# Summing the squares of the queries from 32 rows a head instead of 64

## The chip, the core and the metric

One core of a Trainium2 chip runs the whole program. The metric is the device time of one execution in microseconds. TensorE (PE) multiplies matrices, VectorE (DVE), ScalarE (ACT) and GpSimd (POOL) work element by element, and SyncE (SP) issues most of the DMA transfers. Each engine works through its own queue in order.

## The reference

One layer of an encoder over 1024 tokens of width 1024, in float32. What matters here is the start of its mixer:

```python
h = rmsnorm(x, ln1_g[l]) * (1.0 + sc1) + sh1
p = h @ w_in[l]
q, k, v, cb, cc, cx, ga, gb = jnp.split(p, split_at, axis=-1)
q = rmsnorm(q.reshape(b, s_len, SB_HEADS, SB_HEAD_DIM), q_norm_g[l])   # 16 heads of 64
...
y_a = stick_breaking_attention(q, k, v)
```

`rmsnorm` divides each head's 64 numbers by the root of the mean of their squares. Behind it come the attention, a short gated convolution, a merge by gates, an output projection and a gated feed-forward layer.

## The kernel before

A float32 product is made of three matmuls of 128 rows by 512 columns in the type `float32r`: a matrix is split into a high part (`hi`, a rounding copy by ScalarE) and the rest (`lo`, a subtraction by VectorE), and hi·hi, hi·lo and lo·hi are added up in PSUM (`half_prod`, lines 127 to 129).

The stages follow one another: the values `v` and keys `k` by tokens; then 20 "gates", each of which makes a 2x2 block of a projection by Strassen's scheme with seven products of 12 matmuls (the loop over `gates`); then the attention, with the convolution's projections as filling; the merge, the output projection and the feed-forward layer.

Gates 0 to 3 (`sec == 5`) make the queries, transposed: channels on the partitions, tokens along the columns. Gate j gives four chunks of 128 channels (two heads) by 512 tokens: `c11` is (m = j, n = 0), `c12` is (j, 1), `c21` is (j + 4, 0), `c22` is (j + 4, 1). For the gates' weights, POOL makes four sums of two raw tiles (`s1` to `s4`); `g_split` (lines 524 and, for the subtraction, 133) splits them into `whi` and `wlo`, of which seven pairs exist at a time. The two raw tiles are a ring that SP's queue refills when their last reader is through.

`put_q` takes one chunk `c`. ScalarE scales it into `hi` (line 690), VectorE makes `lo` (691), and both are stored to `d_q` from ScalarE's queue (696). Then ScalarE squares the chunk in place (692), rounds it into `sh` (693), and VectorE takes the rest into `sl`. `sum_q` (line 701) adds up the squares of each head over its 64 partitions: a matmul whose stationary operand is a window of `sel`, a matrix of zeros with a column of ones for either half of the partitions, so that two rows of the 16-row sum `ssq[n]` receive the two heads of chunk m and the other rows a zero:

```python
nc.tensor.matmul(ssq[n], sel[:, 14 - 2 * m:30 - 2 * m], t, start=(nss[n] == 0), stop=(nss[n] == 15))
```

Sixteen chunks with two parts each give 32 such products. `end_q` turns the sums and makes the factors `rq` that the attention's sigmoid uses as its scale.

Order: the code calls `later()` four times a gate, which takes a chunk from `pend` to `put_q`, and a finished pair of squares from `pmm` to `sum_q`. Apart from that, a planner fixes each engine's order when the program is built: among the instructions that are ready by its own reckoning of time, the one that stands first in the program goes first. In this stage no order is written out by hand.

SBUF is handed out in pools. At its bottom lies an area for the descriptors of the DMAs that POOL issues (16 KB of each partition before). POOL issues the 16 loads `ad<-ada` of `mods_last` during the attention and the last seven stores `d_f<-fs`.

Of the kernel before, what the change touches and what calls it, by code (L numbers as in the profile page):

```python
# [9 lines left out]
F32 = mybir.dt.float32  # L10
F32R = mybir.dt.float32r
AF = mybir.ActivationFunctionType
ALU = mybir.AluOpType
# [4 lines left out]
P = 128  # L18
# [4 lines left out]
DH = 64  # L23
# [7 lines left out]
def block_kernel(tc, x, x_t, cols, ada_1, ada_2, ada_row, w_q, w_kv, w_cg, w_a, w_b, w_o, w_g, w_u, w_d, out):  # L31
    nc = tc.nc
    st = ExitStack()
    const = st.enter_context(tc.tile_pool(name="const", bufs=1, reuse_waits="tile"))
# [5 lines left out]
    def nm(s):  # L40
        uid[0] += 1
        return f"{s}_{uid[0]}"
# [45 lines left out]
    one = const.tile([P, 1], F32, name="one")  # L88
    nc.vector.memset(one, 1.0)
    nc.scalar.activation(one, one, AF.Silu)  # L90
    sel0 = const.tile([P, 30], F32, name="sel0")
    nc.vector.memset(sel0, 0.0)
    nc.vector.memset(sel0[:DH, 14:15], 1.0)
    nc.vector.memset(sel0[DH:, 15:16], 1.0)
    sel = const.tile([P, 30], F32R, name="sel")
    nc.scalar.activation(sel, sel0, AF.Copy)
    nhalf = const.tile([P, 8], F32, name="nhalf")
    nc.vector.memset(nhalf, -0.5)
# [33 lines left out]
    def tt(eng, out, a, b, op):  # L132
        eng.tensor_tensor(out=out, in0=a, in1=b, op=op)  # L133
# [195 lines left out]
    for whole in (1, 1, 0, 0, 1, 1, 0, 1, 1, 1, 1):  # L329
        for e in range(2 - whole):  # L330
            r = slice(0, P) if whole else slice(64 * e, 64 * e + 64)
# [188 lines left out]
    def g_split(src):  # L520
        split_at.append(split_at.pop(0))
        hi, lo = (split_at[0].tile([P, 512], F32R, tag=t_, bufs=GS if split_at[0] is gw else GS2, name=nm(t_))
                  for t_ in ("whi", "wlo"))
        nc.scalar.activation(hi, src, AF.Copy)  # L524
        tt(nc.vector, lo, src, hi.bitcast(F32), ALU.subtract)
        return hi, lo
# [7 lines left out]
    def two_raw(g):  # L534
        sec, j = gates[g]
        return g_raw(w_of(sec, j)), g_raw(w_of(sec, j + 4))
# [65 lines left out]
    def g_prod(w, q):  # L602
        ps = g_bank()
        half_prod(ps, w, *fac[q])
        return ps
# [12 lines left out]
    gp = sg_.enter_context(tc.tile_pool(name="phg1", bufs=1, reuse_waits="tile"))  # L618
# [55 lines left out]
    def g_ss():  # L674
        return ps_tr()

    ssq = [g_ss()[:H] for n in range(2)]
    ml = mods_later()
    uu = []
    nss = [0, 0]  # L680
    ccs = {}

    def g_tile():
# [1 line left out]

    def put_q(c, m, n):

        sq2, hl_ = (gp.tile([P, 2, 512], F32R, tag=t_, bufs=b_, name=nm("gt")) for t_, b_ in (("sq", 3), ("tr", 2)))
        hi, lo, sh, sl = hl_[:, 0], hl_[:, 1], sq2[:, 0], sq2[:, 1]
        nc.scalar.activation(hi, c, AF.Identity, scale=qgc)  # L690
        nc.vector.scalar_tensor_tensor(out=lo, in0=c, scalar=qgc, in1=hi.bitcast(F32), op0=ALU.mult, op1=ALU.subtract)
        nc.scalar.activation(c, c, AF.Square)
        nc.scalar.activation(sh, c, AF.Copy)
        tt(nc.vector, sl, c, sh.bitcast(F32), ALU.subtract)
        for e, t in ((0, hi), (1, lo)):
            nc.scalar.dma_start(d_q[e][m, :, n * 512:(n + 1) * 512], t.bitcast(F32))
        pmm.append((m, n, sh, sl))

    def sum_q(m, n, *sq):
        for t in sq:  # L700
            nc.tensor.matmul(ssq[n], sel[:, 14 - 2 * m:30 - 2 * m], t, start=(nss[n] == 0), stop=(nss[n] == 15))
            nss[n] += 1

    def end_q():

        ss = [g_tile()[:H] for n in range(2)]
        for n in range(2):
            nc.scalar.activation(ss[n], ssq[n], AF.Copy)
        yield
        tr = g_bank()  # L710
        for i in range(8):
            nc.tensor.transpose(tr[:, i * H:(i + 1) * H], ss[i // 4][:, i % 4 * P:(i % 4 + 1) * P], ident[:H, :H])
        ms = gp.tile([P, 8, H], F32, name="ms16")
        nc.vector.tensor_scalar(out=ms.rearrange("p i h -> p (i h)"), in0=tr[:, :8 * H], scalar1=1.0 / DH, scalar2=EPS,
                                op0=ALU.mult, op1=ALU.add)
        for i in range(8):
            for h in range(0, H, 8):
                yield
                nc.gpsimd.tensor_tensor(out=rq[:, 0, i, h:h + 8], in0=ms[:, i, h:h + 8], in1=nhalf, op=ALU.pow)
        nc.vector.tensor_scalar(out=rq[:, 1], in0=rq[:, 0], scalar1=-1.0, scalar2=None, op0=ALU.mult)  # L720

    def put_u(c, m, n):

        if not uu:
            uu.extend(g_big() for e in range(2))
            for e in range(2):
                nc.vector.memset(uu[e][:, :2], 0.0)
        u = uu[m // 4]
        s = n * 512
        tt(nc.vector, u[:, 2 + s:514 + s], c, ccs[m, n], ALU.mult)  # L730
        if n == 0:
            uc[m] = True
        elif not uc.get(m):
            raise ValueError(m)
        y = g_tile()
        nc.scalar.activation(y, u[:, s + 2:s + 514], AF.Copy, scale=cw[:, m, 2:3])
        nc.vector.scalar_tensor_tensor(out=y, in0=u[:, s + 1:s + 513], scalar=cw[:, m, 1:2], in1=y, op0=ALU.mult, op1=ALU.add)
        nc.vector.scalar_tensor_tensor(out=y, in0=u[:, s:s + 512], scalar=cw[:, m, 0:1], in1=y, op0=ALU.mult, op1=ALU.add)
        nc.scalar.dma_start(d_y[m, :, s:s + 512], y)

    uc = {}
    pend, pmm, eq = [], [], end_q()
    with tc.high_priority(), tc.issue_after(last_raw[0].ins):
        nc.sync.dma_start(ft[6].bitcast(F32), d_t[6])
    for g, (sec, j) in enumerate(gates):
        raw, raw2 = raws
        p1, p2 = pre[g] if g in pre else (g_prod(g_split(raw[:, :512]), 0), g_prod(g_split(raw[:, 512:]), 1))
        a11, a12, a21, a22 = raw[:, :512], raw[:, 512:], raw2[:, :512], raw2[:, 512:]
        s1, s2_, s3, s4 = (gp2.tile([P, 512], F32, tag=f"ws{q}", bufs=1, name=nm("ws")) for q in range(4))
        with tc.high_priority() if g == 0 else ExitStack():  # L750
            tt(nc.gpsimd, s3, a11, a21, ALU.subtract)
            tt(nc.gpsimd, s2_, a22, s3, ALU.subtract)
            w6 = g_split(s2_)
        tt(nc.gpsimd, s1, a21, a22, ALU.add)
        ws4 = nc.gpsimd.tensor_tensor(out=s4, in0=a12, in1=s2_, op=ALU.subtract)
        if g + 1 < len(gates):
            raws = two_raw(g + 1)
        c11, c21, c12, c22 = (gp.tile([P, 512], F32, tag=f"c{q}", bufs=2, name=nm("c")) for q in range(4))

        def put(c, m, n):  # L760
            if sec == 5:
                pend.append((c, m, n))
            elif sec > 2:
                nc.scalar.activation(c, c, AF.Sigmoid)
                nc.scalar.dma_start((d_sga, d_sgb)[sec - 3][m, :, n * 512:(n + 1) * 512], c)
            elif sec == 1:
                ccs[m, n] = c
            elif n == 1 and m >= 4:
                ccs["late"] = c
            else:  # L770
                put_u(c, m, n)
                if n == 0 and m >= 4:
                    put_u(ccs["late"], m, 1)

        def later():
            if len(pmm) > 2 or pmm and not pend:
                sum_q(*pmm.pop(0))
            if pend:
                put_q(*pend.pop(0))
            elif g > 3 and not pmm:  # L780
                with tc.issue_after(ws4.ins):
                    next(eq, None)

        nc.scalar.activation(c11, p1, AF.Copy)
        p4 = g_prod(g_split(a22), 3) if g + 1 == len(gates) else None
        p6 = g_prod(w6, 5)
        tt(nc.vector, c21, p6, c11, ALU.add)
        tt(nc.vector, c11, p2, c11, ALU.add)
        put(c11, j, 0)
        later()  # L790
        p5 = g_prod(g_split(s1), 4)
        tt(nc.vector, c12, p5, c21, ALU.add)
        p3 = g_prod(g_split(s4), 2) if g == 0 else None
        p7 = g_prod(g_split(s3), 6)
        tt(nc.vector, c22, p7, c12, ALU.add)
        put(c22, j + 4, 1)
        later()
        tt(nc.vector, c21, p7, c21, ALU.add)
        p3 = p3 or g_prod(g_split(s4), 2)
        tt(nc.vector, c12, p3, c12, ALU.add)  # L800
        put(c12, j, 1)
        later()
        p4 = p4 or g_prod(g_split(a22), 3)
        tt(nc.vector, c21, p4, c21, ALU.add)
        later()
        put(c21, j + 4, 0)
        if g + 1 == len(gates):
            for _ in eq:
                pass
        for _ in range((3 if sec in (3, 4) else 0) if g + 1 < len(gates) else 50):  # L810
            next(ml, None)
# [505 lines left out]
    for ch in range(2):  # L1317
# [21 lines left out]
        for i in (0, 4, 1, 2, 3, 5, 6, 7) if ch else range(8):  # L1339
            n, t0 = i // 4, (i % 4) * P  # L1340
# [37 lines left out]
            r = rstd_of(ss, 1.0 / D, dp, 1)  # L1378
# [412 lines left out]
```

## Time and profile before

| | |
|---|---|
| time, median of 3 runs | 1793.43 us (1792.55 to 1795.24) |
| the profiled execution's own time | 1792.41 us |
| its span, first to last instruction | 1790.4 us |
| instructions | 24937 |
| busy: PE, DVE, ACT, POOL | 1782.5, 1273.5, 830.9, 345.0 us |
| selecting products (line 701) | 32, from 220.1 to 298.4 us |

In the lines of the profile, a group reads: line, engine, operation, written tile <- read tiles, shapes, count. In the timeline the first two numbers are start and duration in us, and square brackets hold the idle time before it with what ended it. In the windows each engine has its busy time and the count of instructions. A wait reads: who <- for whom, us in total, times, longest. A busy TensorE is not one at its peak: matmuls overlap, and their pitch, not their duration, is what one costs.

### The profile page before, as it was taken

The numbers are of one execution on the slowest core, as the hardware profiler recorded it, in microseconds if no ns is written. First come the engines' busy times: TensorE is split into PE (matmuls) and PEld (weight loads), VectorE is DVE, ScalarE is ACT, GpSimd is POOL, SyncE is SP. The second block draws the span as 40 slices with busy tenths as digits, with TensorE's granted clock in tenths as the row PEclk, the third lists the DMA queues.
The fourth block names the chain that finished last, engine by engine and source line by source line (L and its number), as shares of the span: only waits on it lengthen the run. The fifth ranks groups of instructions, "written<-read, shape, count | busy, mean of one in ns | idle before, by whom it ended". The sixth has DMA issues, their size and how long they took to land.

```text
span 1790.4 us, 24937 instructions
## 1 busy us (share of the span) xinstructions
PE 1782.5 (100%) x8611; PEld 1485.4 (83%) x8611; DVE 1273.5 (71%) x2030; ACT 830.9 (46%) x1555; POOL 345.0 (19%) x437
## 2 busy tenths in 40 slices
PE   9999999999999999999999999999999999999999
PEld 7888877888888888888888888888888888888887
DVE  6876586777874678777786864698867777644876
ACT  5534364333433567776675221764544444422321
POOL 0024334734231334333332100100000000000000
PEclk9999999999999999999999999999999999999999
DMA  9479654222634977796655856424534344389876
GB/s 383 162 248 381 240 185 165 77 94 100 225 130 147 298 197 191 218 324 172 166 136 176 308 194 212 129 95 169 208 130 148 147 183 157 137 316 345 276 236 220
DMA packets 165010, 359.09 MB, mean 201 GB/s; under 512 B 15538, under 2 KB 60938, under 8 KB 163732
## 3 DMA queue, kind: packets, MB, share of 16 engines
q1 hardware_dynamic: 128300, 289.65, 49.1%
q10 hardware_dynamic: 33096, 55.25, 8.7%
q0 software_dynamic: 3488, 12.59, 2.0%
q8 instruction: 69, 1.13, 0.3%
q14 instruction: 57, 0.47, 0.1%
HBM read 247.84 MB, written 109.62 MB: 200 GB/s over the span
## 4 chain that ended last, share of the span: by engine, by line
PE 96%; DMA 1%; DVE 1%; issue 0%; ACT 0%; POOL 0%; SPq 0%; POOLq 0%; DVEq 0%; ACTq 0%
PE e L129 8%; PE e L128 8%; PE e L127 8%; PE pj L127 7%; PE pj L128 7%; PE pj L129 7%; PE pj L294 7%; PE pj L1026 5%; PE pj L1028 5%; PE pj L1027 5%; PE e L1618 4%; PE e L1619 4%; PE e L1620 4%; PE tr L950 3%; PE o L966 2%; PE z L921 2%
## 5 line engine op out<-in xcount | busy, mean ns | idle before, releaser
L1234 ACT ACTIVATE whi<-raw 128x512 fp32r<-128x512 f32 x137 | 84.9, 628 | 160.6 <-PE e L128 99.8
L1235 DVE TENSOR_TENSOR wlo<-raw,whi 128x512 fp32r<-128x512 f32 x137 | 93.1, 687 | 70.6 <-ACT whi L1234 53.1
L133 POOL TENSOR_TENSOR pt<-pt 128x63 f32<-128x63 f32 (+7 forms) x128 | 101.6, 794 | 212.1 <-DVE pt L936 195.7
L128 PE MATMUL e<-big,whi 128*128 128x512 f32 x352 | 136.9, 389 | 0.0
L127 PE MATMUL e<-big,whi 128*128 128x512 f32 x352 | 136.5, 390 | 0.0
L129 PE MATMUL e<-big,wlo 128*128 128x512 f32 x352 | 136.1, 389 | 0.0
L294 PE MATMUL pj<-whi,big 128*128 128x512 f32 x448 | 132.6, 393 | 0.6 <-ACT big L263 0.4
L133 DVE TENSOR_TENSOR c<-pj,c 128x512 f32<-128x512 f32 x140 | 93.7, 684 | 53.9 <-PE pj L129 53.3
L954 DVE TENSOR_TENSOR atl<-tr,ath 128x512 fp32r<-128x512 f32 (+1 forms) x192 | 104.1, 553 | 35.6 <-ACT ath L953 34.2
L127 PE MATMUL pj<-big,whi 128*128 128x512 f32 x320 | 124.9, 390 | 0.0
L129 PE MATMUL pj<-big,wlo 128*128 128x512 f32 x320 | 124.7, 390 | 0.0
L128 PE MATMUL pj<-big,whi 128*128 128x512 f32 x320 | 124.6, 389 | 0.0
L1619 PE MATMUL e<-wlo,f 128*128 128x512 f32 (+1 forms) x319 | 121.9, 382 | 0.0
L1618 PE MATMUL e<-whi,f 128*128 128x512 f32 (+1 forms) x319 | 121.7, 382 | 0.0
L1620 PE MATMUL e<-whi,f 128*128 128x512 f32 (+1 forms) x319 | 121.6, 382 | 0.0
L923 ACT ACTIVATE pt<-z,rq 128x128 f32<-128x128 f32 (+1 forms) x192 | 107.2, 578 | 26.3 <-PE z L922 23.8
L524 ACT ACTIVATE whi<-raw 128x512 fp32r<-128x512 f32 x108 | 67.5, 629 | 109.0 <-PE pj L128 54.3
L133 DVE TENSOR_TENSOR wlo<-raw,whi 128x512 fp32r<-128x512 f32 x108 | 89.4, 831 | 36.2 <-ACT whi L524 36.1
L1026 PE MATMUL pj<-big,whi 128*128 128x512 f32 x256 | 113.3, 442 | 0.0
L953 ACT ACTIVATE ath<-tr 128x512 fp32r<-128x512 f32 (+1 forms) x192 | 93.2, 488 | 31.8 <-PE tr L950 30.8
L127 PE MATMUL e<-rh,whi 128*128 128x512 f32 x264 | 102.7, 389 | 0.0
L128 PE MATMUL e<-rl,whi 128*128 128x512 f32 x264 | 102.7, 389 | 0.0
(304 smaller groups left out, 4756.1 us busy)
## 6 DMA issues: line engine op xcount, KB each, us to landing
f<-d_f SPq DMA_DIRECT2D x77, 512.0 KB, 4.2
d_f<-fs SPq DMA_DIRECT2D x70, 512.0 KB, 2.6
raw<-w_cg SPq DMA_DIRECT2D x40, 512.0 KB, 4.1
raw<-w_u SPq DMA_DIRECT2D x26, 512.0 KB, 4.5
raw<-w_g SPq DMA_DIRECT2D x25, 512.0 KB, 3.4
raw<-w_kv SPq DMA_DIRECT2D x20, 512.0 KB, 5.2
ld<-ada SPq DMA_DIRECT2D x16, 512.0 KB, 8.7
d_t<-ts SPq DMA_DIRECT2D x16, 512.0 KB, 6.7
```

The lines of the kernel that those rows point to most:

```text
L127: nc.tensor.matmul(ps, wh[:, k, :], fh[:, k, :], start=(k == 0 and not onto), stop=False, skip_group_check=onto)
L128: nc.tensor.matmul(ps, wh[:, k, :], fl[:, k, :], start=False, stop=False, skip_group_check=onto)
L129: last = nc.tensor.matmul(ps, wl[:, k, :], fh[:, k, :], start=False, stop=(k == 3), skip_group_check=onto)
L133: eng.tensor_tensor(out=out, in0=a, in1=b, op=op)
L294: nc.tensor.matmul(ps, a, b, start=(k == 0 and q == 0), stop=(k == KT - 1 and q == 2))
L923: nc.scalar.activation(pt[:, off + s0:off + s0 + m], z[:, :m], AF.Sigmoid, scale=rq[:, 1, i, h:h + 1])
L953: nc.scalar.activation(th[:, :nb, c0:c0 + P], src, AF.Copy)
L954: nc.vector.tensor_tensor(out=tl[:, :nb, c0:c0 + P], in0=src, in1=th[:, :nb, c0:c0 + P].bitcast(F32), op=ALU.subtract)
L1026: nc.tensor.matmul(ps, wh, rh_, start=(k == 0), stop=False)
L1618: nc.tensor.matmul(o, sh, w[0][:, c], start=(j == 0), stop=False)
L1619: nc.tensor.matmul(o, sh, w[1][:, c], start=False, stop=False)
L1620: nc.tensor.matmul(o, sl, w[0][:, c], start=False, stop=(j == NJ - 1))
```

## The change

Two chunks of one gate with the same n, (j, n) and (j + 4, n), share a tile `f` of two halves. ScalarE squares each chunk in four instructions of 32 partitions: the two halves of a head go to the same 32 partitions in the two halves of `f`, so that the four heads of two chunks fill 128 partitions. When both chunks are in, VectorE adds the halves of `f`, and the rounding copy, the subtraction and the two selecting products are made once for the pair. `sel` has four groups of 32 partitions, and its window moves over 22 columns. The square is no longer in place. `later()` keeps one pair back where it kept two chunks. The area for POOL's descriptors is 2 KB of each partition; the two `f` tiles take 8 KB.

```diff
-    sel0 = const.tile([P, 30], F32, name="sel0")
+    sel0 = const.tile([P, 22], F32, name="sel0")
     nc.vector.memset(sel0, 0.0)
-    nc.vector.memset(sel0[:DH, 14:15], 1.0)
-    nc.vector.memset(sel0[DH:, 15:16], 1.0)
-    sel = const.tile([P, 30], F32R, name="sel")
+    for e in range(4):
+        nc.vector.memset(sel0[32 * e:32 * e + 32, 6 + e % 2 + 8 * (e // 2):7 + e % 2 + 8 * (e // 2)], 1.0)
+    sel = const.tile([P, 22], F32R, name="sel")
...
+    folds, nfold = {}, {}
...
     def put_q(c, m, n):
-        sq2, hl_ = (gp.tile([P, 2, 512], F32R, tag=t_, bufs=b_, name=nm("gt")) for t_, b_ in (("sq", 3), ("tr", 2)))
-        hi, lo, sh, sl = hl_[:, 0], hl_[:, 1], sq2[:, 0], sq2[:, 1]
+        hl_ = gp.tile([P, 2, 512], F32R, tag="tr", bufs=2, name=nm("gt"))
+        hi, lo = hl_[:, 0], hl_[:, 1]
         nc.scalar.activation(hi, c, AF.Identity, scale=qgc)
         nc.vector.scalar_tensor_tensor(out=lo, in0=c, scalar=qgc, in1=hi.bitcast(F32), op0=ALU.mult, op1=ALU.subtract)
-        nc.scalar.activation(c, c, AF.Square)
-        nc.scalar.activation(sh, c, AF.Copy)
-        tt(nc.vector, sl, c, sh.bitcast(F32), ALU.subtract)
+        if (m % 4, n) not in folds:
+            folds[m % 4, n] = gp.tile([P, 2, 512], F32, tag="gf", bufs=2, name=nm("gf"))
+        f = folds[m % 4, n]
+        for e in range(4):
+            r = 64 * (m // 4) + 32 * (e // 2)
+            nc.scalar.activation(f[r:r + 32, e % 2], c[32 * e:32 * e + 32], AF.Square)
         for e, t in ((0, hi), (1, lo)):
             nc.scalar.dma_start(d_q[e][m, :, n * 512:(n + 1) * 512], t.bitcast(F32))
-        pmm.append((m, n, sh, sl))
+        nfold[m % 4, n] = nfold.get((m % 4, n), 0) + 1
+        if nfold[m % 4, n] == 2:
+            sq2 = gp.tile([P, 2, 512], F32R, tag="sq", bufs=3, name=nm("gt"))
+            sh, sl = sq2[:, 0], sq2[:, 1]
+            tt(nc.vector, f[:, 0], f[:, 0], f[:, 1], ALU.add)
+            nc.scalar.activation(sh, f[:, 0], AF.Copy)
+            tt(nc.vector, sl, f[:, 0], sh.bitcast(F32), ALU.subtract)
+            pmm.append((m % 4, n, sh, sl))
...
-            nc.tensor.matmul(ssq[n], sel[:, 14 - 2 * m:30 - 2 * m], t, start=(nss[n] == 0), stop=(nss[n] == 15))
+            nc.tensor.matmul(ssq[n], sel[:, 6 - 2 * m:22 - 2 * m], t, start=(nss[n] == 0), stop=(nss[n] == 7))
...
         def later():
-            if len(pmm) > 2 or pmm and not pend:
+            if len(pmm) > 1 or pmm and not pend:
...
-    nc = bacc.Bacc("TRN2", target_bir_lowering=False, num_devices=1)
+    nc = bacc.Bacc("TRN2", target_bir_lowering=False, num_devices=1, dynamic_dma_scratch_size=2048)
```

## The prediction

> **What bounds the kernel now.** I read the page first (busy line, slices, chain), then TensorE's waits, then the stage that the change touches. The page:
>
> ```profile
> PE 1782.5 (100%) x8611; PEld 1485.4 (83%) x8611; DVE 1273.5 (71%) x2030; ACT 830.9 (46%) x1555; POOL 345.0 (19%) x437
> ...
> PE 96%; DMA 1%; DVE 1%; issue 0%; ACT 0%; POOL 0%; SPq 0%; POOLq 0%; DVEq 0%; ACTq 0%
> ```
>
> and the longest entries of the view of TensorE's waits over the whole span:
>
> ```profile
> PE tr L325 <- POOL mk L171: 2.0, 1, 2.0
> PE tr L950 <- POOL pt L133: 0.9, 2, 0.5
> ```
>
> TensorE is busy all the time, 96% of the chain is its own, and its largest wait behind the start is 0.9 us. A matmul taken out therefore shortens the span by its own pitch, as long as nothing else opens a hole; a hole of x us costs x us. The profiled run took 1792.41 us around a span of 1790.4; the median of the three runs, 1793.43, is 1.0 us (0.06%) more. I make the sum on the span and subtract it from the median.
>
> **The stage.** The tile view of `gt` (it takes the `sq`, `tr` and `t` tiles together; count, then shortest, median and longest in ns) lists what a chunk of queries costs, and a line of the view of `c` gives a copy of 128 partitions from PSUM:
>
> ```profile
> L691 DVE SCALAR_TENSOR_TENSOR gt<-c,cst,gt x16: 735/748/1504, 214.4 to 280.4; 128x512 fp32r<-128x512 f32 x16
> L693 ACT ACTIVATE gt<-c x16: 614/618/634, 215.9 to 287.1; 128x512 fp32r<-128x512 f32 x16
> L133 DVE TENSOR_TENSOR gt<-c,gt x16: 678/684/1591, 216.5 to 288.4; 128x512 fp32r<-128x512 f32 x16
> ...
> L708 ACT ACTIVATE gt<-tr x2: 569/578/588, 298.8 to 299.3; 16x512 f32<-16x512 f32 x2
> ```
>
> ```profile
> L784 ACT ACTIVATE c<-pj x20: 577/579/593, 204.2 to 569.4; 128x512 f32<-128x512 f32 x20
> ```
>
> **TensorE: 16 products fewer.** The timeline of TensorE around the last pair of selecting products:
>
> ```profile
> 297.91 0.39 PE L129 MATMUL pj<-big,wlo 128*128 128x512 f32 x1
> 298.14 0.63 PE L701 MATMUL tr<-gt,sel 128*16 128x512 f32 x2
> 298.61 0.39 PE L127 MATMUL pj<-big,whi 128*128 128x512 f32 x1
> ```
>
> A matmul's neighbour starts 0.23 us later (297.91, then 298.14); the pair puts 0.70 us between 297.91 and 298.61, so it costs 0.70 - 0.23 = 0.47, or 0.235 each. Sixteen are 3.76 us. A slot of its 0.39 duration is no price: the matmuls overlap. From above, as an estimate: with the two decimals of these rows 0.01 us off at either end, 0.25 each and 4.0. I take 3.85. This is the one gain.
>
> **ScalarE: 48 squares more, 8 copies fewer.** Each of 16 chunks has four squares of 32 partitions in place of one of 128; a copy is left out in every second chunk. Does a square of 32 partitions cost a quarter? From PSUM, L708 takes 578 ns for 16 partitions and L784 579 ns for 128, both 512 columns wide: the price goes by columns, not partitions. Back to back they start 0.52 or 0.53 us apart (219.40, 219.92, 220.45 below), so 40 more are 40 x 0.52 = 20.8 us; from below, if partitions did count, 48 x 0.13 - 8 x 0.52 = 2.1 us; I take 20.8, nearest to L708.
>
> The Trainium skill ("ScalarE: Activation LUTs", section "What ACT_TABLE_LOAD costs") gives 186 ns + 0.833 ns a column, with 93 ns of overlap back to back, and has no term for partitions; that is an estimate of 612 ns and 519 ns at 512 columns. The trace agrees (median 618 and a pitch of 0.52), and the rule speaks against the change: by it, too, 40 more cost 20.8 us of ScalarE.
>
> Is there room? The windows of the four query gates:
>
> ```profile
> 210.00:230.00 20.00, 20.00 (x90) 16.17 (x89) 15.59 (x23) 11.51 (x19) 7.44 (x5) 1.00 0.62 224
> 230.00:250.00 20.00, 20.00 (x90) 15.71 (x89) 17.79 (x25) 12.48 (x21) 7.19 (x6) 1.00 0.52 171
> 250.00:270.00 20.00, 20.00 (x89) 15.88 (x88) 15.60 (x23) 11.70 (x21) 9.76 (x7) 1.00 0.44 145
> 270.00:290.00 20.00, 20.00 (x90) 15.73 (x89) 15.12 (x23) 11.09 (x19) 2.47 (x3) 1.00 0.61 211
> ```
>
> ScalarE's column sums to 11.51 + 12.48 + 11.70 + 11.09 = 46.8 us of 80. With 20.8 it is 67.6, 84%: on average it fits and costs nothing. If the cover is gone, ScalarE's queue delays the splits of the next weights (`whi`), and TensorE waits for them. Between gates 0 and 1 the cover is thinnest:
>
> ```profile
> 217.62 0.63 ACT L524 ACTIVATE whi<-ws 128x512 fp32r<-128x512 f32 x1 [1.11 <-POOL ws L133]
> 218.77 0.73 ACT L690 ACTIVATE gt<-c,cst 128x512 fp32r<-128x512 f32 x1 [0.52 <-DVE c L133]
> 219.40 0.61 ACT L524 ACTIVATE whi<-ws 128x512 fp32r<-128x512 f32 x1
> ...
> 219.92 0.62 ACT L524 ACTIVATE whi<-ws 128x512 fp32r<-128x512 f32 x1
> 220.45 0.62 ACT L524 ACTIVATE whi<-raw 128x512 fp32r<-128x512 f32 x1
> 221.13 0.64 ACT L524 ACTIVATE whi<-ws 128x512 fp32r<-128x512 f32 x1
> 221.67 0.71 ACT L690 ACTIVATE gt<-c,cst 128x512 fp32r<-128x512 f32 x1
> ...
> 222.28 0.62 ACT L692 ACTIVATE c<-c 128x512 f32<-128x512 f32 x1
> ```
>
> ```profile
> 219.86 0.68 DVE L133 TENSOR_TENSOR c<-pj,c 128x512 f32<-128x512 f32 x1
> ...
> 221.57 1.28 DVE L133 TENSOR_TENSOR wlo<-ws,whi 128x512 fp32r<-128x512 f32 x2
> ```
>
> ```profile
> 220.13 0.62 PE L701 MATMUL tr<-gt,sel 128*16 128x512 f32 x2
> 220.59 0.39 PE L127 MATMUL pj<-ft,whi 128*128 128x512 f32 x1
> ...
> 223.32 0.39 PE L128 MATMUL pj<-ft,whi 128*128 128x512 f32 x1
> ```
>
> By the order of the splits the product that starts at 220.59 uses that of 217.62 and the next, some 2.7 us on at about 223.3, that of 219.40, whose low half VectorE ends at 221.57 + 0.68 = 222.25. So this split may come 1.1 to 1.5 us later, not more. Now the square of a chunk is in place and waits for VectorE's low part (the chunk of 218.77 gets its square only at 222.28), and four splits slip past it. After the change the squares read `c` and write elsewhere, so they are ready as soon as `c` is, stand earlier in the program than gate 1's splits, and I expect them to go first: four of them are 2.1 us, and from 219.40 the split moves to 221.5. Its low half then ends near 222.9, inside a start of about 223.1 (0.2 earlier, as the pair at 220.13 goes), with the low half needed only at the third matmul: a hole of 0 to 0.3 us. I take 0 for the likeliest case.
>
> **Behind gate 1** the splits are early: those of gate 2's sums are made by
>
> ```profile
> 231.65 0.63 ACT L524 ACTIVATE whi<-ws 128x512 fp32r<-128x512 f32 x1 [1.98 <-POOL ws L133]
> ```
>
> ```profile
> 241.08 0.39 PE L127 MATMUL pj<-ft,whi 128*128 128x512 f32 x1
> ```
>
> (ScalarE's, then TensorE's timeline), 9 us ahead of the first product on a summed factor. The raw tiles come later if the last split that reads them does (a ring of two, SP's queue waits for it); the same 9 us cover that.
>
> **VectorE.** Per pair of chunks four instructions before (two low parts at L691, two subtractions at 684 ns), four after (two low parts, an addition, a subtraction): 8 subtractions become 8 additions of the same shape, 0 us. The ring of two folding tiles adds a wait: the first square of a gate needs the tile whose addition, copy and subtraction end the gate before, 0.68 + 0.62 + 0.68 = 2.0 us, three times. ScalarE's splits, ready behind it, fill that; uncovered it is 2.0 us of ScalarE's queue, not of TensorE's. `c` is freed after four squares (2.1 us) where it was freed after square, copy and subtraction (0.62 + 0.62 + 0.68 = 1.9): even. The `d_q` transfers on ScalarE's queue stay 32 and hang on the Identity and its low part as before. Two more memsets of one column for `sel0` stand at the very start, where TensorE waits for POOL's `mk` anyway (the 2.0 us above): 0, or those two instructions if that wait were gone.
>
> **Scratch of 2 KB.** It concerns POOL's transfers alone, and moves every SBUF tile on the left. POOL issues
>
> ```profile
> L644 POOL DMA_DIRECT2D ad<-ada x16: 527/527/538, 967.3 to 1032.9; - x16
> ...
> DMA to landing us min/median/max: 4.2/5.7/6.9
> ```
>
> and seven `d_f` stores near the end. I take 0; it could cost if the smaller area held fewer than the three loads that the three `ad` tiles allow in flight. Place in SBUF shows in no row; I take 0, with 1 us either way.
>
> **Sum:** -3.85 + 0 + 0 + 0 = -3.85 us: 1793.43 - 3.85 = 1789.6 us, -0.21%. A measurement of this kernel can tell about 0.2%, 3.6 us, from no change, so even the full gain is on that edge.
>
> **Rivals.**
> *A, a small hole eats part of the gain.* Identity and four squares of the second chunk (0.52 x 5 = 2.6 us) also get ahead of the split of 219.40: it goes at 221.5 + 2.6 = 224.1, its matmul starts near 225.0 in place of 223.1, a hole of 1.9 us. For it: the second chunk's `c` ends at 219.86 + 0.68 = 220.54, before the first squares are through. Against it: the order of each queue is fixed when the program is built, and there the four splits went before this chunk's Identity (221.67). Time 1793.43 - 3.85 + 1.9 = 1791.5.
> *B, ScalarE becomes the bound: slower.* All three chunks of gate 0 that end together (3 x 2.6 = 7.8 us) pass gate 1's splits: 219.40 + 7.8 = 227.2, low half done near 228.4, a hole of about 5 us; the next gates inherit late raw tiles and lose some 0.5 us each. 3.85 - 5 - 1.5 = -2.7: 1796.1 us. It decides from holes of 3.85 us on. For it: 84% load and in-order queues; against: 9 us of lead behind gate 1, and TensorE can take another ready product in between.
> *C, scratch:* POOL's loads go one by one. Sixteen at 5.7 us to landing are 91 us; they take 1032.9 - 967.3 = 66 now. What waits behind them (the output projection's first weights) could come up to 25 us late; with half of that hidden, 1789.6 + 12.5 = 1802.1. The Trainium skill ("DMA: Bandwidth & Descriptors", section "SWDGE vs HWDGE vs iDMA") has the descriptors of POOL's transfers in rings in SBUF; no run here shows one full. Against it: three loads in flight are few.
> *D, the change does not do what it says* (the products left out are refilled by the queue's own slack): no row speaks for it, TensorE having none.
>
> **How the numbers follow.** Full gain with a hole under 0.3 us: 0.50. A: 0.30. B: 0.15. C: 0.03. D: 0.02. Of the first case, centred on 1789.6, about four fifths fall beyond the 0.2% (under 1789.8, its middle nearly on the line, with later stages reordered by a microsecond either way); I give faster 0.42. B's deeper half and C give slower 0.13; the rest, 0.45, is no change that can be told. The likeliest case alone runs from 1788.4 (4.0 gained, 1 us of place) to 1790.6; the range takes in A and most of B: 1788.4 to 1795.8.
>
> **What would show it.** Right: 16 rows of `sel` products at the same 0.235; 64 squares of 32x512 at about 0.6; ScalarE near 17 of 20 us in the windows from 210 to 290; no TensorE wait on `whi` or `wlo` there. Wrong: TensorE waiting for ScalarE's `whi` or VectorE's `wlo` between 220 and 230 (A, B), squares at a quarter of the time, `ad` issues spread beyond 1033 (C), or a wait of the `sel` products for `gt`.

## The result and the profile after

The changed kernel took 1806.95 us (median of 4 runs, 1805.68 to 1808.13) beside 1793.72 us for the kernel before on the same chip (median of 4, one run more than in the table above): a ratio of 1.0073, 95% interval 1.0056 to 1.0091. It is 13.2 us slower, where 1789.6 was forecast and the range ended at 1795.8. The profiled execution took 1806.78 us around a span of 1804.8, 14.4 more than the span before.

The page of the changed kernel, its busy line and its chain:

```profile
PE 1786.7 (99%) x8595; PEld 1485.3 (82%) x8595; DVE 1276.1 (71%) x2032; ACT 857.9 (48%) x1595; POOL 345.3 (19%) x437
...
PE 92%; ACT 2%; DMA 2%; DVE 2%; issue 1%; SPq 0%; POOL 0%; ACTq 0%; POOLq 0%; DVEq 0%
```

The 16 products are gone (8595 matmuls in place of 8611), and still TensorE is busy for longer and holds less of the chain. Its waits over the whole span say where to look:

```profile
PE pj L723 <- ACT gt L719: 4.8, 1, 4.8
PE tr L712 <- DVE gt L133: 2.3, 1, 2.3
PE pj L127 <- ACT whi L524: 2.1, 1, 2.1
PE tr L325 <- POOL mk L171: 2.0, 1, 2.0
PE tr L961 <- POOL pt L133: 2.0, 3, 1.4
```

Three of them are new and lie in the query gates or just behind them. The windows (columns: span; busy time of TensorE, weight loads, VectorE, ScalarE, POOL with their counts; TensorE's clock; DMA) show them beside ScalarE's load:

```profile
220.00:240.00 20.00, 17.94 (x79) 14.26 (x78) 16.78 (x24) 18.55 (x32) 6.85 (x5) 1.00 0.53 172
240.00:260.00 20.00, 20.00 (x90) 16.02 (x89) 16.74 (x22) 18.45 (x31) 6.32 (x4) 1.00 0.44 147
260.00:280.00 20.00, 17.74 (x78) 13.97 (x77) 15.96 (x22) 16.00 (x27) 6.20 (x4) 1.00 0.53 183
280.00:300.00 20.00, 20.00 (x89) 15.78 (x88) 12.89 (x20) 14.01 (x24) 0.92 (x1) 1.00 0.50 184
300.00:320.00 20.00, 15.24 (x60) 11.85 (x59) 10.98 (x15) 6.36 (x12) 13.83 (x10) 0.83 0.32 106
```

TensorE loses 2.06, 2.26 and 4.76 us there, and in the last window the clock is 0.83 as well: the stretch behind the third hole is run at half speed.

**The first hole**, between gates 0 and 1, in the timelines of POOL, ScalarE and TensorE:

```profile
216.43 1.29 POOL L133 TENSOR_TENSOR ws<-raw 128x512 f32<-128x512 f32 x1
217.68 1.30 POOL L133 TENSOR_TENSOR ws<-raw,ws 128x512 f32<-128x512 f32 x1
```

```profile
217.76 0.64 ACT L524 ACTIVATE whi<-ws 128x512 fp32r<-128x512 f32 x1 [0.76 <-POOL ws L133]
218.58 0.73 ACT L691 ACTIVATE gt<-c,cst 128x512 fp32r<-128x512 f32 x1 [0.19 <-DVE c L133]
219.33 1.92 ACT L698 ACTIVATE gf<-c 32x512 f32<-32x512 f32 x3
...
221.26 0.63 ACT L698 ACTIVATE gf<-c 32x512 f32<-32x512 f32 x1
221.91 0.63 ACT L524 ACTIVATE whi<-ws 128x512 fp32r<-128x512 f32 x1
```

```profile
220.15 0.39 PE L129 MATMUL pj<-big,wlo 128*128 128x512 f32 x1
222.60 0.50 PE L127 MATMUL pj<-ft,whi 128*128 128x512 f32 x1 [2.06 <-ACT whi L524]
```

An Identity and four squares stand ahead of the split of 221.91; before, the Identity alone did, and the split was made at 219.40. And that split is the one that gate 1's first product on a factor (`ft`) needs: `p6` reads the split of `s2_` = `a22 - s3`, the sum with a raw tile and a `ws` tile for operands, which POOL starts at 217.68. The split of 217.76 belongs to the sum of raw alone (`s1`). It is done at 218.40, but the product that reads it stands behind `p6` in TensorE's queue, so TensorE waits all the same.

The three squares from 219.33 and the fourth at 221.26 start 0.64 us apart. The median of all such pairs in the stage is 0.64 too, while the splits behind them (221.91, 222.45, 222.97, 223.50) start 0.52 to 0.54 apart. So a square of 32 partitions lasts no longer than an instruction of 128, but it costs ScalarE's queue 0.12 us more, because the next instruction does not overlap it.

**The second hole** parts the two selecting products of one pair. VectorE's, POOL's and TensorE's timelines:

```profile
270.40 1.78 DVE L133 TENSOR_TENSOR wlo<-raw,whi 128x512 fp32r<-128x512 f32 x1
272.10 1.75 DVE L133 TENSOR_TENSOR gt<-gf,gt 128x512 fp32r<-128x512 f32 x1
```

```profile
269.89 1.74 POOL L133 TENSOR_TENSOR ws<-raw,ws 128x512 f32<-128x512 f32 x1
271.71 1.59 POOL L766 TENSOR_TENSOR ws<-raw,ws 128x512 f32<-128x512 f32 x1
```

```profile
273.90 0.40 PE L712 MATMUL tr<-gt,sel 128*16 128x512 f32 x1 [2.26 <-DVE gt L133]
```

The second product waits for the subtraction of 272.10, which stands behind a `wlo`. Both take some 1.1 us longer than the median of 0.69, and both run beside POOL's sums; together that is about as long as the hole. No run moved POOL's sums alone, so this is read, not tested.

**The third hole** goes back to POOL, which got its raw tiles late. POOL before the change, then POOL, ScalarE and TensorE after it:

```profile
287.88 1.30 POOL L133 TENSOR_TENSOR ws<-raw,raw 128x512 f32<-128x512 f32 x1 [17.53 <-DMA raw<-w_cg]
```

```profile
299.08 1.29 POOL L133 TENSOR_TENSOR ws<-raw,raw 128x512 f32<-128x512 f32 x1 [25.78 <-DMA raw<-w_cg]
```

```profile
301.62 0.63 ACT L524 ACTIVATE whi<-ws 128x512 fp32r<-128x512 f32 x1 [7.17 <-POOL ws L133]
...
304.43 1.05 ACT L719 ACTIVATE gt<-tr 16x512 f32<-16x512 f32 x2
```

```profile
299.91 0.39 PE L129 MATMUL pj<-big,wlo 128*128 128x512 f32 x1
305.05 0.61 PE L723 MATMUL pj<-dm,gt 16*128 16x16 f32 x4 [4.76 <-ACT gt L719]
...
306.18 0.63 PE L128 MATMUL pj<-big,whi 128*128 128x512 f32 x1
306.61 0.63 PE L129 MATMUL pj<-big,wlo 128*128 128x512 f32 x1
```

The transposes (`pj<-dm,gt`) wait for two copies of 16x512, which stand in ScalarE's queue behind splits of sums that POOL started at 299.08, 11.2 us later than before. The load that POOL waits for was itself issued 10.3 us later; SP's queue, before and after:

```profile
283.57 0.33 SPq L513 DMA_DIRECT2D raw<-w_cg  x1
```

```profile
293.84 0.33 SPq L513 DMA_DIRECT2D raw<-w_cg  x1
```

It waited for the low part of the last split that reads the tile, which ScalarE made at 292.47 in place of 282.19, behind the squares of gate 3. After the hole the matmuls start 0.43 us apart in place of 0.23, until 310.86.

The starts of the first matmul of each stage give a table of stages, in us, from the profiled run of each kernel. "Gates" is from the first gate product to the first `z` of the attention, "FFN" its gate and up products:

| kernel | gates | attention | out-projection | FFN | profiled run us | median us |
|---|---|---|---|---|---|---|
| before | 401.5 | 467.2 | 92.5 | 420.7 | 1792.41 | 1793.72 |
| after | 412.4 | 468.0 | 93.1 | 422.8 | 1806.78 | 1806.95 |
| e1_place | 403.8 | 469.8 | 93.1 | 422.8 | 1799.92 | 1798.78 |
| e12_place_both | 401.5 | 467.2 | 92.5 | 420.7 | 1791.98 | 1792.82 |
| e3_aligned | 411.7 | 473.6 | 92.5 | 420.7 | 1808.41 | 1803.79 |
| e4_high_only | 397.7 | 470.2 | 92.5 | 420.7 | 1791.77 | 1789.88 |
| e5_one_square | 398.2 | 469.7 | 92.5 | 420.7 | 1791.31 | 1791.31 |
| e9_raw_three | 398.4 | 472.4 | 92.5 | 420.7 | 1794.35 | 1793.11 |
| e13_before_three | 401.6 | 468.9 | 92.5 | 420.7 | 1794.63 | 1793.34 |
| e15_change_three | 402.0 | 469.8 | 93.1 | 422.8 | 1797.57 | 1797.57 |

The gates lose 10.9 us; but the FFN, some 870 us behind the last selecting product, loses 2.1 as well, with no hole at all. That is a second cause, and the first to be taken apart. Where the profiled run lies above the median, most of all in e3_aligned, its stages are longer than the usual run's.

### The profile page after: what moved, and what is told of

Read it like the earlier page. It is cut to its first block, busy times and chain, and to the rows that moved or that the text cites. A ratio compares the mean times of both kernels' runs of the same rounds, so it can differ in the third digit from the quotient of the medians.

```text
span 1804.8 us, 24939 instructions
## 1 busy us (share of the span) xinstructions
PE 1786.7 (99%) x8595; PEld 1485.3 (82%) x8595; DVE 1276.1 (71%) x2032; ACT 857.9 (48%) x1595; POOL 345.3 (19%) x437
## 4 chain that ended last, share of the span: by engine, by line
PE 92%; ACT 2%; DMA 2%; DVE 2%; issue 1%; SPq 0%; POOL 0%; ACTq 0%; POOLq 0%; DVEq 0%
PE pj L294 8%; PE e L127 8%; PE e L129 8%; PE e L128 8%; PE pj L127 6%; PE pj L129 6%; PE pj L128 6%; PE pj L1037 4%; PE pj L1039 4%; PE pj L1038 4%; PE e L1629 4%; PE e L1631 4%; PE e L1630 4%; PE tr L961 3%; PE o L977 2%; PE z L932 2%
```

## The experiments

All medians stand beside runs of the kernel before on the same chip, 1793.1 to 1793.4.

**Place in SBUF, and scratch.** The two `sel` tiles are 32 B shorter each, so all pools on the left side start 64 B lower relative to those on the right. The kernel before with that shift alone:

```diff
-PADL, PADR = 192, 224
+PADL, PADR = 128, 224
```

> The kernel before with its padding on the left of SBUF 64 B smaller, so that every tile of the left pools starts 64 B lower, as after the change, while the right pools stay; the order of every engine is that of before. Theory of place: the mean pitch of the products whose two operands lie on different sides rises as it did after the change (gate products on factors 226.8 to 231.4 ns, output projection on low weights 227.0 to 230.9, FFN 226.6 to 227.8), and the time by 4 to 6 us: 1797.5 to 1799.5. Rival (only the order of ScalarE and its holes made the kernel slower, the pitch rose because of other engines' traffic): 1793.7, within 0.5 us, pitches as before.

Measured: 1798.78 us, ratio 1.0029 (1.0018 to 1.0041). The 1848 products of the FFN, first and last, in the timeline of TensorE before and with the shift:

```profile
1155.78 0.39 PE L127 MATMUL e<-big,whi 128*128 128x512 f32 x1
...
1576.25 0.39 PE L129 MATMUL e<-rh,wlo 128*128 128x512 f32 x1
```

```profile
1160.82 0.39 PE L127 MATMUL e<-big,whi 128*128 128x512 f32 x1
...
1583.39 0.39 PE L129 MATMUL e<-rh,wlo 128*128 128x512 f32 x1
```

420.47 us become 422.57 with the same instructions in the same order. The gate products on factors, which have one operand on either side, go from 226.7 to 230.0 ns from start to start (mean from 310 to 500 us), the FFN's from 226.7 to 227.8. The gate products on `big`, with both operands on the left, keep their 226.7. Place costs 5.4 us here.

Then the right side moved by the same 64 B:

```diff
-PADL, PADR = 192, 224
+PADL, PADR = 128, 288
```

> The kernel before with the left pools 64 B lower, as in the run of place alone, and the right pools 64 B lower too, so that the distance between the two sides is that of before, modulo 256. Theory: the products slow down by the distance between what two engines or two operands read, so pitches and time return: 1793.3 within 0.7 us. Rival (it is the address of a tile itself, modulo 256, that counts): the pitch of gate products on factors stays at 231 or rises further, and the time is 1798 or more.

Measured: 1792.82 us, ratio 0.9995 (0.9986 to 1.0004), the pitch on factors 226.7 ns. So it is the distance between the two sides that counts here, not the address of a tile.

The scratch of 2 KB alone, in the kernel before:

```diff
-    nc = bacc.Bacc(..., num_devices=1)
+    nc = bacc.Bacc(..., num_devices=1, dynamic_dma_scratch_size=2048)
```

> The kernel before with descriptor scratch of 2 KB alone: the left pools move by 14,336 B, a multiple of 256. Theory: POOL's loads of ad still keep three in flight and the place modulo 256 is that of before, so 1793.7 within 1 us. Rival C of the prediction (POOL's loads go one by one): the ad loads spread beyond 1033 us and the time rises by up to 12 us. Rival on place (any shift matters): a pitch change and some us in either direction.

Measured: 1793.34 us, ratio 1.0000 (0.9991 to 1.0008). The scratch costs nothing, though it moves the left side by 14,336 B: not every distance matters.

The changed kernel with the place put right:

```diff
-PADL, PADR = 192, 224
+PADL, PADR = 256, 224
```

> The changed kernel with 64 B more padding on the left, so that the left pools start where they did before, modulo 256. Theory of place plus bursts: pitches return to 226.5 to 227 ns and the time falls by 4 to 6 us to about 1802, still 8 us above the kernel before, because the three holes of TensorE (2.1, 2.3, 4.8 us) and the slow clock behind the last stay. Rival (place is nothing): 1807 as it was, pitches still 231.

Measured: 1803.79 us (1800.99 to 1808.41), ratio 1.0053 (1.0040 to 1.0067): 10.5 us above the kernel before on its chip in place of 13.2, so 2.8 us back, less than the 4 to 6 expected. The intervals overlap, so by the times alone this could be noise; the stages show it, with out-projection and FFN exactly as before. The wide spread is seen in the trace of the slowest run, which is the profiled one. TensorE behind the first hole, and the windows there:

```profile
221.96 0.50 PE L127 MATMUL pj<-ft,whi 128*128 128x512 f32 x1 [2.05 <-ACT whi L524]
```

```profile
222.00:224.00 2.00, 2.00 (x7) 1.66 (x8) 2.00 (x4) 2.00 (x5) 0.00 (x0) 0.79 0.97 321
224.00:226.00 2.00, 2.00 (x6) 1.51 (x6) 1.09 (x2) 1.96 (x5) 0.00 (x0) 0.50 0.65 204
```

Here a hole of 2.05 us is followed by 3.4 us at half clock, which cost 1.6 us more; in the changed kernel's own profile a hole of 2.06 us at the same place was not. The mean clock of the five runs orders their times: 0.998 gives 1801.0 and 1801.8, 0.996 gives 1803.8, 0.995 gives 1806.5, 0.994 gives 1808.4.

**The price of a product.** The kernel before with the high products alone, so the low part of the squares is left out of the sum:

```diff
-        for t in sq:
+        for t in sq[:1]:
```

> The kernel before with the selecting products of the high parts alone, 16 in place of 32 (the low part of the squares is left out of the sum; it is still computed). ScalarE and VectorE have the load of before; the planner's order of the queues behind the first selecting product is another one. Theory: the price of a product was right, so the time falls by 3.5 to 4 us, to about 1790, if the new order opens no hole of its own. Rival (the products left out were cover for something else): within 1 us of 1793.7, with new waits of TensorE in the trace.

Measured: 1789.88 us (1788.44 to 1793.53), ratio 0.9984 (0.9975 to 0.9993). The gates are 3.8 us shorter: the price was right. The attention gave some back in the profiled run, at its start. VectorE there, with the high products alone and then before:

```profile
597.43 0.69 DVE L133 TENSOR_TENSOR vb<-vb,va 128x512 f32<-128x512 f32 x1 [3.61 <-DMA vb<-d_v]
```

```profile
598.17 0.69 DVE L133 TENSOR_TENSOR vb<-vb,va 128x512 f32<-128x512 f32 x1 [0.68 <-DMA vb<-d_v]
```

The gates end 3.7 us sooner, but the load of `vb` lands only 0.7 us sooner (though issued 5.0 us sooner), and TensorE waits 3.2 us for what VectorE and POOL do behind it. This was read, not tested.

**Squares or fold?** Realigned, one square of 128 partitions a chunk, so the halves of a head are not folded and the sums are other numbers; addition, copy, subtraction, ring and 16 products stay:

```diff
-        for e in range(4):
-            r = 64 * (m // 4) + 32 * (e // 2)
-            nc.scalar.activation(f[r:r + 32, e % 2], c[32 * e:32 * e + 32], AF.Square)
+        nc.scalar.activation(f[:, m // 4], c, AF.Square)
```

> The changed kernel with the left pools realigned (64 B of padding), and one square of 128 partitions a chunk in place of four of 32 (so the halves of a head are not folded and the sums are other numbers); folding addition, copy, subtraction, ring of two folding tiles and 16 products stay. ScalarE has 48 instructions, some 25 us, less. Theory (the extra squares in ScalarE's queue make the holes): none of the three holes stays, 1793.3 - 3.8 = 1789.5, up to 1791. Rival (the holes come of the fold itself, its longer chain of addition, copy and subtraction and the later sums): holes of 2 us and more before a selecting product and before the end of the sums, 1795 or more.

Measured: 1791.31 us, ratio 0.9988 (0.9980 to 0.9997), the gates 398.2 us. TensorE's waits in that kernel:

```profile
PE tr L959 <- POOL pt L133: 2.9, 2, 2.4
PE tr L325 <- POOL mk L171: 2.0, 1, 2.0
PE o L975 <- DVE atl L963: 0.7, 1, 0.7
```

No hole is left in the gates: with a ring of two raw tiles, the extra squares make the holes, not the fold. What keeps the time above 1789.5 is, by the trace, the same wait at the start of the attention (2.9 us).

**Order of the queue.** Realigned, the splits of the gates at high priority:

```diff
+        with tc.high_priority() if len(split_at) > 1 else ExitStack():
             nc.scalar.activation(hi, src, AF.Copy)
             tt(nc.vector, lo, src, hi.bitcast(F32), ALU.subtract)
```

> The changed kernel, realigned, with the splits of the gates' weights planned at high priority. In ScalarE's order the split of gate 1's first product then stands behind the Identity and one square of c22 in place of four. Theory: the first hole falls from 2.0 to about 0.5 us, with no slow clock behind it; the third, made by POOL's sums and late raw tiles, shrinks only if the late splits of the gates go earlier too: 1798 to 1802 where the realigned kernel alone has 1803.8. Rival (priority moves the same work elsewhere): 1803 to 1806.

Measured: 1798.13 us (1797.17 to 1803.51), ratio 1.0029 (1.0018 to 1.0040). In the profiled run, the slowest of seven, the first hole is gone; the waits for selecting products are 3.4 us, again behind VectorE instructions of 1.77 and 1.76 us beside POOL's sums, and the third hole is 2.1.

The end of the sums a gate later, realigned:

```diff
-            elif g > 3 and not pmm:
+            elif g > 4 and not pmm:
```

> The changed kernel, realigned, with the end of the sums (copies of 16x512, transposes) allowed one gate later, from the sixth gate on. Theory: the third hole (3.1 us realigned, 4.8 before that) and the half clock behind it (some 2.6 us) go, since the transposes no longer stand in TensorE's order before copies that queue behind waiting splits: 1797 to 1799. Rival (TensorE would wait for the late splits of that gate in any case): a hole of 2 us or more on whi at the same place, 1802 or more.

Measured: 1804.69 us, ratio 1.0059 (1.0046 to 1.0071). The theory missed: the hole moved a gate on and grew.

```profile
PE pj L723 <- ACT gt L719: 5.8, 1, 5.8
```

ScalarE's and POOL's timelines show why:

```profile
315.98 0.63 ACT L524 ACTIVATE whi<-ws 128x512 fp32r<-128x512 f32 x1 [4.75 <-POOL ws L133]
...
320.05 0.57 ACT L719 ACTIVATE gt<-tr 16x512 f32<-16x512 f32 x1
```

```profile
313.43 1.29 POOL L133 TENSOR_TENSOR ws<-raw,raw 128x512 f32<-128x512 f32 x1 [8.31 <-DMA raw<-w_cg]
```

The raw tiles are still late one gate on, because each load waits for the late split of the gate before. The copies are only what stands behind that. Both edits together:

> Both edits, splits at high priority and the end of the sums a gate later, realigned. Theory: holes 1 and 3 gone, at most the second (1.9 us with a slow clock of 1.7) left: 1791 to 1796. Rival: other waits take their place, 1798 or more.

Measured: 1798.66 us, ratio 1.0027 (1.0016 to 1.0039), no better than the priority alone: missed too, the second hole 2.7 us and the third 1.6.

**The ring of raw tiles.** Realigned, three raw tiles in place of two:

```diff
-    GR, NG, GS, GS2 = 2, 2, 4, 3
+    GR, NG, GS, GS2 = 3, 2, 4, 3
```

> The changed kernel, realigned, with a ring of three raw weight tiles in place of two. Theory: the third hole begins at the raw tiles, whose loads wait for the last late split of the gate before; with a third tile POOL's sums for the gate behind the queries come back from 299 us towards 288, and the hole before the end of the sums with its half clock goes: 1803.8 - 3.1 - 2.6, about 1798; holes one and two stay. Rival (the copies of 16x512 simply stand badly in ScalarE's order): the hole stays though POOL's sums are early, 1802 or more.

Measured: 1793.11 us, ratio 0.9998 (0.9989 to 1.0006), 10.7 us under the realigned kernel and far more than expected. Its windows:

```profile
220.00:240.00 20.00, 20.00 (x89) 16.34 (x88) 16.42 (x26) 19.70 (x34) 7.79 (x5) 1.00 0.42 154
...
260.00:280.00 20.00, 20.00 (x89) 16.12 (x89) 14.66 (x23) 18.63 (x32) 6.31 (x5) 1.00 0.40 150
300.00:320.00 20.00, 20.00 (x90) 16.57 (x89) 15.44 (x21) 6.27 (x11) 19.21 (x13) 1.00 0.12 40
```

ScalarE is fuller than in the changed kernel (19.7 of 20 us) and TensorE has no hole. POOL starts gate 1's sums at

```profile
202.55 1.29 POOL L133 TENSOR_TENSOR ws<-raw,raw 128x512 f32<-128x512 f32 x1 [0.63 <-DVE wlo L133]
```

12 us sooner than the 214.70 of the changed kernel, so gate 1's splits are made ahead of the first squares. Nor does any of the eight subtractions that the selecting products wait for run beside a sum of POOL's (0.68 to 0.69 us each). The load of ScalarE did no harm by itself; the lead was too short for the bursts.

The ring and the priority, realigned, both edits as above:

> The ring of three raw tiles and the splits at high priority together, realigned. Theory: holes one and three gone, the second (2.7 us before a selecting product) left: 1792 to 1796, where splits first alone has 1798.1. Rival (ScalarE is full at 18 to 19 of 20 us, so any order leaves some hole): 1797 or more.

Measured: 1792.55 us, ratio 0.9995 (0.9986 to 1.0003), gates 398.0 us, but the stage ahead of them ends 3 us later, with new waits for `vs`.

The ring alone in the changed kernel, not realigned, and the ring in the kernel before:

> The changed kernel with the ring of three alone, its left pools 64 B off as the change has them. Theory (holes through the ring and place add up): the holes go, the place stays with its 3 to 5 us: 1796 to 1799. Rival (at slower products the splits have more time, so place and holes overlap): 1793 to 1795; or (the 64 B opens holes of its own): 1801 or more.

> The kernel before with a ring of three raw weight tiles (and the scratch of 2 KB that makes room for it). Theory: TensorE has no hole in its gates, so a longer ring has nothing to give there: 1793.4, within 1 us; the gate stage lasts the 401.5 us of before, where the folding with the same ring had 398.4. Rival (the ring itself is the gain of the run with three tiles, or it costs in later stages): 1791 or less, or 1795 or more.

Measured: 1797.57 us, ratio 1.0025 (1.0016 to 1.0034), and 1793.34 us, ratio 1.0001 (0.9992 to 1.0009). The two causes add up, as far as the spread (1793.89 to 1801.75) lets one see: each beside the kernel before on its own chip, the ring takes 9.0 us of the 13.2 away and the place 4.6 more. In the kernel before a third tile is worth nothing, as it has no hole to fill. With equal rings the fold's gates are 3.2 us shorter (398.4 and 401.6), yet the medians are equal (1793.11, 1793.34): in the profiled runs its attention took 3.5 us more, in part again behind `vb` (waits of 1.6 us, 0.8 with the ring alone), in part by a hole of 1.3 us further on with a stretch at half clock.

**Another way to fold.** Realigned, one square in place and the move by transfers:

```diff
+        nc.scalar.activation(c, c, AF.Square)
         for e in range(4):
             r = 64 * (m // 4) + 32 * (e // 2)
-            nc.scalar.activation(f[r:r + 32, e % 2], c[32 * e:32 * e + 32], AF.Square)
+            nc.gpsimd.dma_start(f[r:r + 32, e % 2], c[32 * e:32 * e + 32])
```

> The changed kernel, realigned, with one square of 128 partitions a chunk, in place, and the move of its four blocks of 32 partitions into the folding tile by transfers that POOL issues (64 of 64 KB); the sums are those of the changed kernel. Theory: with ScalarE's 48 extra squares gone the 16 products fewer are gained in full, and the later sums have slack: 1789.5 to 1792. Rival (the 4 MB and POOL's 64 issues delay the weight sums that POOL also makes, or chunks held longer delay the next gate): holes on ws or raw, 1794 or more.

Measured: 1811.12 us, ratio 1.0097 (1.0082 to 1.0113). The rival held. TensorE's waits:

```profile
PE pj L127 <- ACT whi L524: 4.0, 3, 2.4
PE tr L713 <- DVE gt L133: 3.5, 5, 1.8
PE tr L713 <- ACT gt L707: 3.5, 2, 1.9
```

POOL's load doubles in the windows from 240 to 280 us (13.4 of 20), and the sums come too late for their products.

Two versions are under the kernel before by more than their interval, and neither makes the full sums: the one with the high products alone, by 3.5 us, leaves out the low part of the squares, and the one with a single square a chunk, by 1.8 us, adds up other numbers. With the sums complete, the best (three raw tiles, realigned, with the priority or without) is level with the kernel before.

## Why the prediction was wrong

- **TensorE, -3.85 us: right.** The gates of the high products alone are 3.8 us shorter, those of one square 3.3, those of the fold with equal rings 3.2.
- **ScalarE's price, "40 x 0.52 = 20.8 us": mis-sized.** The 64 squares last 0.613 to 0.635 us each, by columns, not partitions, as forecast. But they start 0.64 us apart, not 0.52: the pitch was taken from copies of 128 partitions. ScalarE's busy time rose by 27.0 us (830.9 to 857.9), and four squares cost 2.6 us in place of 2.1. Why they do not overlap is open; one square of 128 partitions does (0.52 to 0.55 us to the next instruction).
- **"Between gates 0 and 1 ... a hole of 0 to 0.3 us": failed.** The order was foreseen, the squares do pass the split, and it moved from 219.40 to 221.91 near the 221.5 forecast. What was wrong is which product reads it. "The product that starts at 220.59 uses that of 217.62" was taken from the order of the splits; by operands it is the split of 219.40, done at 220.01. The slack was 0.6 us, not 1.1 to 1.5. Nor did TensorE "take another ready product in between": it stood idle up to 222.60, though the split of `s1` was done at 218.40. The hole was 2.06 us.
- **"Behind gate 1 ... the same 9 us cover that": failed, and cost most.** The 9 us were the lead of one split in one gate; there they held, gate 2 has no hole. In a ring of two, a load waits for the last split that reads the tile, POOL for the load, and ScalarE's next splits for POOL, so a late split comes back in later gates. POOL's sums came 4.8 us late at 252.51, 3.1 at 267.02 and 11.2 at 299.08; the last holds TensorE's own first two holes too. With a third tile all three holes go. "On average it fits" was true, and beside the point.
- **VectorE, 0 us: failed, 2.26 us.** The prediction counted VectorE's instructions at their median. The second selecting product of a pair waits for its subtraction (the wait of `sel` products for `gt` named as a sign of error), and that and the `wlo` before it are stretched to 1.75 and 1.78 us beside POOL's sums. With one square a chunk it does not occur.
- **Place, "I take 0, with 1 us either way": mis-sized.** It is 2.8 to 5.4 us by three pairs of kernels. No row of the trace before could show it.
- **The clock was no term of the sum.** Behind the third hole TensorE ran at half clock to 310.86: by the pitches some 2.5 us.
- **Scratch, 0: right.** Rival C is out.
- **Rival B** had the sign and the mechanism (squares ahead of splits, late raw tiles), but 6.5 us of holes in place of 9.1 with 2.5 of clock; and full ScalarE was not its condition, as the run with three raw tiles shows.

The sum over the gates: -3.8 (products) + 2.3 (place) + 9.1 (holes) + 2.5 (clock, an estimate) = 10.1, beside 10.9 measured; out-projection and FFN add 0.6 + 2.1 by place, the attention 0.8. Together they are the 14.4 us of the profiled span; the medians differ by 13.2.

## What to carry to other kernels

Work moved onto an engine that is half idle is free only if its bursts fit into the lead of what is queued behind it: find by its operands which product reads the delayed tile, and follow the delay through the ring that feeds it, for it comes back in later gates. A longer ring gave back more than any reordering. Price an instruction by its start-to-start time, measured on its own shape. After any change of a tile's size, check the pitch of matmuls far from the change: if it moved, restore the tiles' addresses with padding before judging the edit.

## What the runs showed of the hardware

- The pitch of matmuls depends on the distance between their tiles in SBUF: 64 B off, gate products with operands on both sides took 230.0 ns in place of 226.7, and moving both sides together brought 226.7 back. A shift of 14,336 B changed nothing. Why is open; no other distance was tried.
- Squares of 32 partitions start 0.64 us apart on ScalarE, where splits, and squares of 128 partitions with the next instruction, start 0.52 to 0.55 apart; each lasts 0.61 to 0.64.
- An addition or subtraction of VectorE lasts longer beside one of POOL's. In the changed kernel from 210 to 300 us those that ran without one took at most 0.70 us, and the seven that took 1.13 to 1.78 us all ran beside one. Many ran beside one and were not stretched.
- A hole of about 2 us in TensorE may cost another three quarters of its length in clock (1.6 us in the realigned kernel). Half clock came in stretches of 3.4 or 6.8 us. Holes of 1.88 and 2.05 us (realigned), 1.63 (both edits) and 1.27 (three raw tiles) were followed by 3.4 us of it; holes of 2.06 and 2.26 us (changed kernel), 2.70 (both edits) and even 3.16 (high products alone) by none; holes of 3.07 us (realigned) and 4.76 (changed kernel) by the 6.8, which began inside the hole. The Trainium skill ("TensorE: Matmul & The Clock Gate", section "What's actually happening") has a free-running window of about 3.4 us and lets the clock fall after at least one idle window. The stretches at half clock and the chance in them agree; the length needed does not: 1.3 us were enough here.
